# A hybrid attention and linear-attention layer on one core: the token scales stored once instead of tile by tile, and four weight roundings moved from VectorE to ScalarE

## The chip, the core and the metric

The kernel runs on one core of a Trainium2 chip. The metric is the device time of one execution in microseconds (us). Engines are named as in the profile: PE is TensorE (the matrix unit), DVE is VectorE, ACT is ScalarE, POOL is GpSimd, SP is SyncE. In this kernel SP issues every DMA.

## The reference

One inference step of one layer, for a prompt of 2048 tokens of width 1024 and for 32 sample tokens that continue another stream:

```
n = rmsnorm(x, g_mix)
z = n @ w_in                       # 1024 -> 2320 columns: qa 512, ka 128, va 128,
                                   # qg 256, kg 256, vg 512, rg 512, ca 16
A = sliding-window attention(qa, ka, va)     # chunks of 64, window 128, sinks, QK-norm
G = gated linear attention(qg, kg, vg, log_sigmoid(ca @ w_alpha + b_alpha) / 16)
G = rmsnorm(G) * silu(rg)
h = x + concat(A, G) @ w_out
y = h + relu(rmsnorm(h) @ w_up)^2 @ w_down   # 1024 -> 4096 -> 1024
```

Besides y, the last keys and values and the states of the linear attention are returned. All is float32. The RMS norm of a token is a number per token (the token scale, `rstd`) times the gain `g_mix` per column; the kernel multiplies the activations by the gain ahead of the projection and the products by the token scale behind it.

## The kernel before

The prompt is cut into 16 tiles of 128 tokens, and the 32 sample tokens are tile 16. A matrix product in float32 is made of three products of rounded parts: each operand is split into `hi` (rounded to the format of the fast matmul) and `lo` (the rest, rounded), and PE computes hi·hi + hi·lo + lo·hi. For a weight (`split_weight`, lines 195 to 208), SP loads a piece of 512 KB into a buffer `stage`, one engine rounds it to `hi` (ACT in line 203 or DVE in line 205), and another writes `lo` (POOL or DVE in line 207).

The kernel has three phases.

Attention takes up to some 392 us of the trace. Its tiles come in the order 0 to 9, 16 (sample), 10 to 15. For each tile, `front` (lines 252 to 275) loads the transposed tokens `xT1a` (512 KB), has DVE multiply them by the gain, ACT round them to `nT_h` and POOL write `nT_l`; `scales` (line 280) loads the tokens a second time (`x1a`) and has DVE compute the 128 token scales into column t of the tile `rstd`, which has 128 partitions and 17 columns; `store` (lines 282 to 288) writes to DRAM what the second phase reads again: the scales of the tile (line 285) and, after every second tile, `nT_h` and `nT_l` of two tiles (1 MB each). Then PE computes the projections of the tile (`zq`, `zkv`, `zr`), and the attention of the tile (`qTp`, `S`, `pT`, `O` on PE) follows as a task that is resumed between matmuls.

The store of line 285 takes one column of `rstd`: 128 partitions with 4 bytes each, written to a DRAM tensor `rs` of its own, of shape [128, 1]. The second phase needs the scales along the free axis, the same for all partitions: line 631 reads the tensor back as one row of 512 bytes, broadcast to 128 partitions of the tile `rb`. The products `kq` of the linear attention multiply by it (line 739).

Linear attention takes from 392 to some 760 us. Its weights (`wqg`, `wkg`, `wvg0`, `wvg1`, each of two pieces) are loaded by `prepare_gla` (line 612): `wqg`, `wkg`, `wvg0` after the projection of keys and values of tile 15, `wvg1` some work later. The table `GLA_ENG` (line 594) says who splits the two pieces of a weight: the first is rounded by ACT and its `lo` written by POOL; the second has both done by DVE. The feed-forward network takes the rest, up to the end.

What sets the order: PE's instructions are chained by hand in the order in which the program issues them (`_pe`), and tasks are resumed by an estimated clock that each matmul advances. The order on the other engines is made by a scheduler at build time. Every engine then works strictly in order. SP issues DMAs in order too, and a DMA is given one of 8 semaphores in rotation, so each DMA waits until the one issued 8 before it on SP has landed. Loads `xT1a`, `x1a`, `stage` and the tiles `sq` and `rg` share a pool of 5 buffers of 512 KB, so a load may also wait until the last reader of an older tile is done.

Of the kernel before, what the change touches and what calls it, by code (L numbers as in the profile page):

```python
# [9 lines left out]
F32 = mybir.dt.float32  # L10
F32R = mybir.dt.float32r
I32 = mybir.dt.int32
AF = mybir.ActivationFunctionType
# [6 lines left out]
P = 128  # L20
# [8 lines left out]
class Builder:  # L29
    def __init__(self, ctx, tc, a, o, nt=NT, ffn=True):  # L30
        self.ctx, self.tc, self.nc, self.a, self.o = ctx, tc, tc.nc, a, o
        self.nt, self.with_ffn = nt, ffn
        nc = self.nc
        self.V, self.S, self.G, self.T, self.Q = nc.vector, nc.scalar, nc.gpsimd, nc.tensor, nc.sync
        pool = lambda name, bufs, **kw: ctx.enter_context(tc.tile_pool(name=name, bufs=bufs, **kw))
        self.const = pool("const", 1)
        self.small = pool("small", 3)
        self.io = pool("io", 5)
        self.w = pool("w", 8)
        self.dram = pool("dram", 1, space=DRAM)  # L40
        self.psm = pool("psm", 3, space=PSUM)
        self.pss = pool("pss", 5, space=PSUM)
        tiles = list(range(nt)) + [nt]
        dt = lambda shape, name: self.dram.tile(shape, F32, tag=name, name=name)
        self.mixT = [dt([P, KB, self.rows(t)], f"mixT{t}") for t in tiles]

        self.nTd = [[dt([P, KB, 2 * P if t < nt else NS], f"nT{x}{t}") for x in "hl"] for t in range(0, nt + 1, 2)]
        self.cad = [dt([16, self.rows(t)], f"ca{t}") for t in tiles]
        self.rsd = [dt([self.rows(t), 1], f"rs{t}") for t in tiles]
        self.rgd = [dt([self.rows(t), 512], f"rgd{t}") for t in tiles]  # L50

        self.last_pe = self.last_table = None
        self.clock = 0.0
        self.state_clock = -1e9
        self.tasks = []
        self.seq = 0
# [174 lines left out]
    def attention_phase(self):  # L231
        tc, a, V, S, G, Q = self.tc, self.a, self.V, self.S, self.G, self.Q
        nt = self.nt
        w_in = a["w_in"].rearrange("(k p) n -> p k n", p=P)
        with ExitStack() as ctx:
            wx = ctx.enter_context(tc.tile_pool(name="wx1a", bufs=1))
            wk = ctx.enter_context(tc.tile_pool(name="wk1a", bufs=2))
            c = ctx.enter_context(tc.tile_pool(name="c1a", bufs=1))
# [14 lines left out]
            def front(t, xT=None):  # L253

                r = self.rows(t)
                xT = xT or load_xT(t)
                if t == nt:
                    nT[t] = (*(c.tile([P, KB, NS], F32R, tag=f"nTs{x}", name=f"nTs{x}") for x in "hl"), 0)
                elif t % 2 == 0:
                    nT[t] = (*self.tok_pair(f"nT_{t}", 2 * P), 0)  # L260
                else:
                    nT[t] = (*nT[t - 1][:2], P)
                h, l, off = nT[t]
                ts = slice(off, off + r)
                step = 2 if t == 0 else 4
                for k in range(0, KB, step):
                    ks = slice(k, k + step)
                    V.tensor_tensor(
                        out=xT[:, ks], in0=xT[:, ks], in1=self.gmix[:, ks].unsqueeze(2).broadcast_to([P, step, r]), op=ALU.mult
                    )  # L270
                    S.activation(h[:, ks, ts], xT[:, ks], AF.Copy)
                    (V if t in (0, nt) else G).tensor_tensor(
                        out=l[:, ks, ts], in0=xT[:, ks], in1=h[:, ks, ts].bitcast(F32), op=ALU.subtract
                    )

            def scales(t, x=None):

                r = self.rows(t)
                x = x or load_x(t)
                V.tensor_copy(self.rstd[:r, t : t + 1], self.rms(x, x, r, f"a{t}"))  # L280

            def store(t):

                r = self.rows(t)
                Q.dma_start(self.rsd[t], self.rstd[:r, t : t + 1])
                if t == nt or t % 2:
                    for x, dst in zip(nT[t], self.nTd[t // 2]):
                        Q.dma_start(dst, x.bitcast(F32))
# [3 lines left out]
            gm = slice(self.g0, self.g0 + KB)  # L292
            Q.dma_start(self.packed[:, gm], a["packed"][:, gm])
            V.memset(self.ones, 1.0)
            S.activation(self.rstd[:, :1], self.ones, AF.Square)
            front(order[0])
            wq = self.wide_pairs(w_in, 0, "wq", (("act", "dve", 2), ("act", "dve", 2)), (0,))
# [29 lines left out]
            def project_q(t):  # L327
                r = self.rows(t)
                rs = self.rstd[:r, t : t + 1]
                qk = wk.tile([P, 5, 2, 64], F32, tag="qk", name=f"qk_{t}", bufs=3)  # L330
                sq = self.io_tile(f"sq_{t}")[:, :640].rearrange("p (j v d) -> p j v d", j=5, v=2)
                ps = self.ps_m(f"zq_{t}")[:r]
                token_gemm(ps, t, wq)
                pv = ps.rearrange("p (v j d) -> p j v d", v=2, j=4)
                S.activation(qk[:r, 0:4], pv, AF.Copy, scale=rs)
                S.activation(sq[:r, 0:4], pv, AF.Square, scale=rs)
                return qk, sq
# [31 lines left out]
            def project_gate(t):  # L369

                r = self.rows(t)
                rg = self.io_tile(f"rg_{t}")[:r, :512]
                ps = self.ps_m(f"zr_{t}")[:r]
                token_gemm(ps, t, wr)
                V.tensor_scalar(out=rg, in0=ps, scalar1=self.rstd[:r, t : t + 1], scalar2=None, op0=ALU.mult)
                Q.dma_start(self.rgd[t], rg)
# [180 lines left out]
            for i, t in enumerate(order):  # L557
                for j in order[i + 1 : i + 2 + (nt in order[i + 1 : i + 2])]:
                    if j not in nT:
                        front(j)  # L560
                        scales(j)
                        store(j)
                if i == 0:
                    z = {j: project_q(j) for j in order[:2]}
                    z = {j: project_kv(j, *z[j]) for j in z}
                    with tc.issue_after(self.weights_in):
                        for j in order[:2]:
                            store(j)
                elif i > 1:
                    z[t] = project_kv(t, *project_q(t))  # L570
                if t == nt - 1:
                    self.prepare_gla(0)
                self.spawn(attend_sample(*z.pop(t)) if t == nt else attend(t, *z.pop(t)))
                if t != nt - 2:
                    project_gate(t)
                if t == nt - 1:
                    project_gate(t - 1)
                if t == nt:
                    self.load_gla_consts()
# [11 lines left out]
            self.finish()  # L591


    GLA_ENG = (("act", "pool"), ("dve", "dve"))

    def load_gla_consts(self):
        a, c, Q, V = self.a, self.mid, self.Q, self.V
# [14 lines left out]
    def prepare_gla(self, part):  # L612
        w_in = self.a["w_in"].rearrange("(k p) n -> p k n", p=P)
        if part == 0:
            self.wqg = self.cols_pair(w_in, 768, "wqg", self.GLA_ENG)
            self.wkg = self.cols_pair(w_in, 1024, "wkg", self.GLA_ENG)
            self.wvg = self.wide_pairs(w_in, 1280, "wvg", self.GLA_ENG, (0,))
        else:
            self.wvg += self.wide_pairs(w_in, 1280, "wvg", self.GLA_ENG, (1,))

    def gla_tokens(self, h, tiles):
        nt = self.nt
        pair = self.tok_pair(f"nTb_{h}", sum(self.rows(t) for t in tiles))
        rb = self.mid.tile([P, 288], F32, tag="rb", name=f"rb_{h}")
        off = 0
        for t in tiles:
            r = self.rows(t)
            if t == nt or t % 2 == 0:
                for x, src in zip(pair, self.nTd[t // 2]):
                    self.Q.dma_start(x[:, :, off : off + src.shape[2]].bitcast(F32), src)  # L630
            self.Q.dma_start(rb[:, off : off + r], self.rsd[t].rearrange("r o -> o r").broadcast_to([P, r]))
            off += r
        return pair, off, rb

# [810 lines left out]
```

## Time and profile before

| what | us |
|---|---|
| median of 3 runs | 2317.13 (2316.85 to 2319.09) |
| the profiled execution | 2316.26 |
| its span, first to last instruction | 2314.5 |
| PE busy in the span | 2253.7 (97%) |
| DVE busy | 1410.0 (61%) |
| ACT busy | 953.1 (41%) |
| POOL busy | 1197.4 (52%) |
| mean granted clock of PE | 0.98 of full speed |

The profile is of one execution. Busy time is the time in which an engine executes something. PE is busy nearly all of the span, so it is PE's idle time, 61 us in all, and the stretches in which its granted clock is low that other engines and DMAs can change. A row of a timeline gives the start, the duration and the instruction, and in brackets how long the engine was idle before it and what released it. That releaser is inferred: where the engine named had been done for long, another wait ended last.

### The profile page before, as it was taken

To read this page: it belongs to the slowest core of one execution; us is meant where nothing else is said; L and a number is where in the kernel's file an instruction comes from. 1 tells how busy PE (TensorE), PEld (TensorE's weight loads), DVE (VectorE), ACT (ScalarE), POOL (GpSimd) and SP (SyncE) were. 2 spreads that over 40 slices of the span, in tenths; PEclk is the share of its full clock that TensorE was granted. 3 is DMA by queue.
4 is the path that set the end of the run, shared out by engine and by line. 5 is a ranking of instruction groups with operands and counts; after the bars stand their busy time and mean duration, and the time that the engine had idled before them with its cause. 6 is when DMAs were issued, how large, how long until landed. Compare 5 with 4: busy or idle time off the path is not lost.

```text
span 2314.5 us, 39745 instructions
## 1 busy us (share of the span) xinstructions
PE 2253.7 (97%) x15389; PEld 2117.4 (91%) x15389; DVE 1410.0 (61%) x3631; ACT 953.1 (41%) x1953; POOL 1197.4 (52%) x995
## 2 busy tenths in 40 slices
PE   7999999899998999999999999999999999999999
PEld 5777776788877999999999999999999999999999
DVE  7666657688887755555553755555554755555555
ACT  3554445455562643333334533333334533333331
POOL 3221224333241396667765566666665386666662
PEclk9999999889988999999999999999999999999999
DMA  8654563221322423222236222222227122222221
GB/s 233 140 107 107 145 173 125 84 73 66 106 82 81 128 78 97 82 74 74 73 109 185 74 73 74 73 73 73 74 63 219 55 74 73 73 74 73 74 64 52
DMA packets 154301, 221.56 MB, mean 96 GB/s; under 512 B 38224, under 2 KB 114976, under 8 KB 150272
## 3 DMA queue, kind: packets, MB, share of 16 engines
q1 hardware_dynamic: 154112, 219.02, 32.2%
q8 instruction: 121, 1.98, 0.4%
q14 instruction: 68, 0.56, 0.1%
HBM read 180.08 MB, written 38.91 MB: 95 GB/s over the span
## 4 chain that ended last, share of the span: by engine, by line
PE 74%; DVE 12%; DMA 5%; POOL 3%; issue 3%; ACT 2%; SPq 1%; POOLq 0%; DVEq 0%; ACTq 0%
PE dn L112 30%; PE PS4B L112 4%; PE PS3T L112 4%; PE PS2T L112 4%; PE PA22T L112 4%; PE PA11B L112 4%; PE PA12B L112 4%; PE PS1T L112 4%; PE zq L112 3%; PE op L112 3%; PE zr L112 3%; DVE AT L892 2%; PE zkv L112 2%; PE zv L112 2%; PE O L112 1%
## 5 line engine op out<-in xcount | busy, mean ns | idle before, releaser
L1103 POOL TENSOR_TENSOR wu<-stage,wu 128x512 fp32r<-128x512 f32 x336 | 432.5, 1299 | 468.3 <-ACT wu L1102 456.6
L1279 DVE TENSOR_TENSOR y<-y,dn 128x360 f32<-128x360 f32 (+1 forms) x768 | 393.0, 514 | 228.4 <-PE dn L112 225.5
L1102 ACT ACTIVATE wu<-stage 128x512 fp32r<-128x512 f32 x336 | 206.2, 628 | 493.6 <-PE dn L112 213.5
L1105 POOL TENSOR_TENSOR stage<-stage 128x512 f32<-128x512 f32 x192 | 249.4, 1299 | 7.5
L1232 ACT ACTIVATE r<-PA11B 128x360 f32<-128x360 f32 (+1 forms) x48 | 22.1, 460 | 284.4 <-PE PA11B L112 284.4
L1217 DVE TENSOR_TENSOR PA12B<-PA12B,r 128x360 f32<-128x360 f32 (+1 forms) x48 | 25.3, 526 | 150.2 <-PE PA12B L112 150.2
L719 POOL TENSOR_TENSOR g<-g,ggla 128x512 f32<-128x512 f32 (+1 forms) x17 | 25.0, 1489 | 170.4 <-ACT g L120 170.4
L112 PE MATMUL PA22T<-T4h,wu 128*128 128x360 f32 (+1 forms) x384 | 101.5, 328 | 0.0
L112 PE MATMUL PS3T<-T3h,wu 128*128 128x360 f32 (+1 forms) x384 | 100.1, 323 | 0.1
L112 PE MATMUL PS4B<-B22h,wu 128*128 128x360 f32 (+1 forms) x384 | 100.2, 324 | 0.0
L112 PE MATMUL PS1T<-T1h,wu 128*128 128x360 f32 (+1 forms) x384 | 98.9, 321 | 0.0
L112 PE MATMUL PA11B<-B11h,wu 128*128 128x360 f32 (+1 forms) x384 | 98.8, 321 | 0.0
L112 PE MATMUL PS2T<-T2h,wu 128*128 128x360 f32 (+1 forms) x384 | 98.7, 320 | 0.0
L112 PE MATMUL PA12B<-B21h,wu 128*128 128x360 f32 (+1 forms) x384 | 98.7, 321 | 0.0
L892 DVE COPY_PREDICATED AT<-masks,A 64x64 f32<-64x64 int32 (+1 forms) x330 | 82.9, 253 | 13.7 <-PE A L112 3.8
L816 POOL TENSOR_TENSOR E<-cc 128x256 f32<-128x256 f32 (+1 forms) x117 | 68.3, 622 | 25.3 <-PE A L112 19.5
L506 ACT ACTIVATE P<-S,negm 128x192 f32<-128x192 f32 (+2 forms) x128 | 51.6, 417 | 51.1 <-DVE negm L501 31.6
L112 PEld LDWEIGHTS PA22T<-T4h,wu 128*128 128x128 f32 x384 | 70.1, 193 | 0.0
L112 PEld LDWEIGHTS PS3T<-T3h,wu 128*128 128x128 f32 x384 | 69.1, 190 | 0.5 <-ACT T3h L1135 0.5
L112 PEld LDWEIGHTS PS4B<-B22h,wu 128*128 128x128 f32 x384 | 69.0, 190 | 0.0
L112 PEld LDWEIGHTS PS1T<-T1h,wu 128*128 128x128 f32 x384 | 68.1, 188 | 0.0
L112 PEld LDWEIGHTS PS2T<-T2h,wu 128*128 128x128 f32 x384 | 68.1, 188 | 0.0
(1008 smaller groups left out, 7736.5 us busy)
## 6 DMA issues: line engine op xcount, KB each, us to landing
stage<-in_w_up SPq DMA_DIRECT2D x96, 512.0 KB, 4.2
stage<-in_w_down SPq DMA_DIRECT2D x96, 512.0 KB, 3.9
stage<-in_w_out SPq DMA_DIRECT2D x24, 512.0 KB, 5.2
xT1a<-in_xT_prompt SPq DMA_DIRECT2D x16, 512.0 KB, 7.5
stage<-in_w_in SPq DMA_DIRECT2D x16, 512.0 KB, 5.3
x1a<-in_x_prompt SPq DMA_DIRECT2D x16, 512.0 KB, 6.9
out_yT_prompt<-y SPq DMA_DIRECT2D x32, 180.0 KB, 4.4
m<-mixT SPq DMA_DIRECT2D x11, 512.0 KB, 4.5
```

What stands on the lines that cost most here:

```text
L112: self._pe(self.T.matmul(out, lhsT, rhs, start=start, stop=stop), ns)
L506: S.activation(Pt[:, u, :n], sp[:, jp], AF.Exp, bias=negm[:, ch, u : u + 1], scale=0.125, accum_out=rsum[:, ch, u : u + 1],)
L719: G.tensor_tensor(out=gv, in0=gv, in1=ggla[:r].unsqueeze(1).broadcast_to([r, 4, P]), op=ALU.mult)
L816: G.tensor_tensor(out=e4, in0=c4, in1=ref, op=ALU.subtract)
L892: V.copy_predicated(dst, mk.unsqueeze(1).broadcast_to([L // nh, 2, w // m, m]), src[r].rearrange("s p (n m) -> s p n m", m=m),)
L1102: self.after(S.activation(h, src, AF.Copy), after)
L1103: G.tensor_tensor(out=l, in0=src, in1=f32(h), op=ALU.subtract)
L1105: tt = lambda o, x, y, op: G.tensor_tensor(out=o, in0=x, in1=y, op=op)
L1217: tt = lambda out, x, y, op=ALU.add: V.tensor_tensor(out=out, in0=x, in1=y, op=op)
L1232: S.activation(r0, product(b, "A11", "B11"), AF.Copy)
L1279: V.tensor_tensor(out=yg[:, f, :], in0=yg[:, f, :], in1=ps, op=ALU.add)
```

## The change

The DRAM tensor of the scales becomes one tensor `rs` of 17 rows and 128 columns. The 17 stores of line 285 go. Instead the tile `rstd` is set to 1.0 as a whole at the start (the sample tile fills 32 of its 128 partitions), and after the projection of keys and values of tile 15, PE transposes `rstd` (128 x 17) into PSUM (17 x 128), ACT copies that to a tile `rsT`, and one DMA writes it to `rs`, 17 rows of 512 bytes. The 17 broadcast loads of `rb` read rows of `rs`.

Apart from this, `GLA_ENG` now has the second piece of each of the four weights rounded by ACT in place of DVE; DVE still writes its `lo`.

```diff
-        self.rsd = [dt([self.rows(t), 1], f"rs{t}") for t in tiles]
+        self.rsd = dt([nt + 1, P], "rs")
...
             def store(t):
-                r = self.rows(t)
-                Q.dma_start(self.rsd[t], self.rstd[:r, t : t + 1])
                 if t == nt or t % 2:
                     for x, dst in zip(nT[t], self.nTd[t // 2]):
                         Q.dma_start(dst, x.bitcast(F32))
...
             V.memset(self.ones, 1.0)
+            V.memset(self.rstd, 1.0)
...
                 if t == nt - 1:
+                    pt = self.ps_s("rsT")[: nt + 1, :P]
+                    self.tr(pt, self.rstd)
+                    rsT = c.tile([nt + 1, P], F32, tag="rsT", name="rsT")
+                    S.activation(rsT, pt, AF.Copy)
+                    Q.dma_start(self.rsd, rsT)
                     self.prepare_gla(0)
...
-    GLA_ENG = (("act", "pool"), ("dve", "dve"))
+    GLA_ENG = (("act", "pool"), ("act", "dve"))
...
-            self.Q.dma_start(rb[:, off : off + r], self.rsd[t].rearrange("r o -> o r").broadcast_to([P, r]))
+            self.Q.dma_start(rb[:, off : off + r], self.rsd[t : t + 1, :r].broadcast_to([P, r]))
```

The change moves instructions at three places that matter below. The first is SP at the start, from the stores of tiles 0 and 1 to the load of tile 2's tokens (`xT1a`; `ck`, `cv`, `wal`, `d`, `masks` are small constant loads). Before:

```order
L285 DMA rs_127<-rstd 128x1
L285 DMA rs_128<-rstd 128x1
L288 DMA nTh_92<-nT_0h 128x2048
L288 DMA nTl_93<-nT_0l 128x2048
L404 DMA ck<-in_cache_k 128x128
L405 DMA cv<-in_cache_v 128x128
L603 DMA wal<-in_w_alpha 16x256
L604 DMA d_2801<-in_resets 128x288
L605 DMA masks<-in_masks 128x224
L631 DMA rb_4265<-rs_127 128x128
L631 DMA rb_4265<-rs_128 128x128
L250 DMA xT1a_510<-in_xT_prompt 128x1024
```

And now, with the load of `gk` that precedes this piece in both kernels:

```order
L315 DMA gk<-in_g_k 128x128
L286 DMA nTh_92<-nT_0h 128x2048
L286 DMA nTl_93<-nT_0l 128x2048
L403 DMA ck<-in_cache_k 128x128
L404 DMA cv<-in_cache_v 128x128
L608 DMA wal<-in_w_alpha 16x256
L609 DMA d_2774<-in_resets 128x288
L610 DMA masks<-in_masks 128x224
L250 DMA xT1a_493<-in_xT_prompt 128x1024
```

The load of `xT1a` stood 8 places behind the store of `nTl`; it now stands 6 behind it and 8 behind the load of `gk`.

The second place is DVE at the end of the attention phase, where the first pieces of the linear attention's weights arrive (`wqgh`, `wqgl`, `wkgh`, `wkgl` are hi and lo of two weights; `ssqk`, `ca`, `qk` belong to the keys and queries of tile 15, `qT` and `caT` to tile 14). Before:

```order
L205 CAST wqgh<-stage 128x1024
L457 TENSOR_SCALAR qT_4011<-qTp_4000,packed 128x4x2x64
L396 COPY caT_4008<-kTp_4005 16x128
L207 TENSOR_TENSOR wqgl<-stage,wqgh 128x1024
L352 TENSOR_REDUCE ssqk_4032<-sq_3925 128x10
L350 TENSOR_SCALAR ca_4030<-zkv_3966,rstd 128x16
L205 CAST wkgh<-stage 128x1024
L353 TENSOR_SCALAR ssqk_4032<-ssqk_4032 128x10
L207 TENSOR_TENSOR wkgl<-stage,wkgh 128x1024
```

And now:

```order
L456 TENSOR_SCALAR qT_3979<-qTp_3968,packed 128x4x2x64
L395 COPY caT_3976<-kTp_3973 16x128
L207 TENSOR_TENSOR wqgl<-stage,wqgh 128x1024
L351 TENSOR_REDUCE ssqk_4000<-sq_3893 128x10
L349 TENSOR_SCALAR ca_3998<-zkv_3934,rstd 128x16
L352 TENSOR_SCALAR ssqk_4000<-ssqk_4000 128x10
```

The two roundings are gone from DVE, and `qT` of tile 14 no longer stands behind one of them; `wkgl` follows five small instructions later.

The third place is ACT in the same stretch (`pS` and `aT` are steps of tile 14's attention; `qk`, `sq`, `v` take the products `zkv` of tile 15; `kW` is its key tile). Before:

```order
L203 ACTIVATE wqgh<-stage 128x1024
L536 ACTIVATE pS_1_128_3993<-pT_1_128_3988 128x512
L536 ACTIVATE pS_1_64_3998<-pT_1_64_3995 128x256
L345 ACTIVATE qk_3924<-zkv_3966,rstd 128x128
L346 ACTIVATE sq_3925<-zkv_3966,rstd 128x128
L348 ACTIVATE v_4028<-zkv_3966,rstd 128x128
L203 ACTIVATE wkgh<-stage 128x1024
L467 ACTIVATE kW_4017<-kTp_4005 128x128
L549 ACTIVATE aT_4091<-O_3945 128x512
```

And now:

```order
L203 ACTIVATE wqgh<-stage 128x1024
L535 ACTIVATE pS_1_128_3961<-pT_1_128_3956 128x512
L535 ACTIVATE pS_1_64_3966<-pT_1_64_3963 128x256
L203 ACTIVATE wqgh<-stage 128x1024
L344 ACTIVATE qk_3892<-zkv_3934,rstd 128x128
L345 ACTIVATE sq_3893<-zkv_3934,rstd 128x128
L466 ACTIVATE kW_3985<-kTp_3973 128x128
L347 ACTIVATE v_3996<-zkv_3934,rstd 128x128
L575 ACTIVATE rsT<-rsT 17x128
L203 ACTIVATE wkgh<-stage 128x1024
L548 ACTIVATE aT_4064<-O_3913 128x512
L203 ACTIVATE wkgh<-stage 128x1024
```

ACT has the second pieces of `wqgh` and `wkgh` and the copy `rsT` between its steps of the attention.

Further on, SP issues the store of `rs` behind tile 15's `v_prompt` store, and the five loads of `rb` for tiles 16 and 0 to 3 directly after it and one weight load and one store (before, they stood far apart and earlier). Late in the linear attention the scheduler swaps some neighbours: on ACT, `kdT` of tile 15 now stands behind the rounding `wo_11h` and one copy `op`, ahead of which it stood. The feed-forward network's order stays as it was but for a few neighbours.

## Rows read from the trace of the kernel before

**Rows 1.** The stages: window; us; busy (count) of each engine; clock; DMA share; GB/s.

```profile
27.00:80.00 53.00, 47.64 (x266) 39.31 (x267) 37.84 (x139) 23.46 (x73) 16.76 (x25) 0.96 0.80 178
80.00:317.00 237.00, 237.00 (x1358) 182.33 (x1357) 150.38 (x583) 116.19 (x375) 56.41 (x96) 0.99 0.50 118
317.00:376.00 59.00, 52.41 (x304) 40.73 (x303) 41.05 (x108) 27.64 (x88) 21.35 (x22) 0.97 0.75 220
...
760.00:2314.50 1554.50, 1543.45 (x9671) 1539.54 (x9669) 862.27 (x1749) 585.89 (x1120) 972.12 (x679) 1.00 0.28 85
```

**Rows 2.** Waits of PE until 760 us: us in total, times, longest.

```profile
PE zq L112 <- ACT nT_2h L271: 2.3, 1, 2.3
...
PE pT L116 <- DVE qT L457: 1.9, 1, 1.9
...
PE zq L112 <- POOL nT_2l L272: 0.7, 1, 0.7
```

**Rows 3.** The chain of waits, 25 to 82 us: start us, us, what.

```profile
30.38 13.50 DMA nTl<-nT_0l
43.95 3.73 DMA xT1a<-in_xT_prompt
```

**Rows 4.** Windows, by stretches of a few us.

```profile
31.00:32.00 1.00, 1.00 (x9) 1.00 (x9) 1.00 (x1) 0.00 (x0) 1.00 (x1) 0.86 3.06 393
32.00:38.00 6.00, 6.00 (x40) 5.46 (x39) 5.61 (x24) 1.77 (x6) 3.24 (x9) 1.00 0.70 27
...
58.00:64.00 6.00, 6.00 (x44) 4.88 (x42) 4.23 (x21) 4.05 (x19) 1.18 (x4) 1.00 0.50 18
...
335.00:342.00 7.00, 7.00 (x48) 5.95 (x48) 2.59 (x9) 2.14 (x4) 0.00 (x0) 1.00 1.02 55
```

**Rows 5.** The seventeen stores of rs, line 285.

```profile
DMA to landing us min/median/max: 2.9/8.8/15.2
```

**Rows 6.** The store of the sample tile alone, at 206.65 us.

```profile
DMA to landing us min/median/max: 2.9/2.9/2.9
```

**Rows 7.** Timeline of DVE at the start: start us, us, line, [idle before <-releaser].

```profile
35.86 0.82 DVE L352 TENSOR_REDUCE ssqk<-sq 128x10 f32<-128x640 f32 x1 [0.32 <-ACT sq L346]
...
47.70 1.29 DVE L268 TENSOR_TENSOR xT1a<-xT1a,packed 128x512 f32<-128x512 f32 x2 [5.15 <-DMA xT1a<-in_xT_prompt]
...
75.78 1.29 DVE L268 TENSOR_TENSOR xT1a<-xT1a,packed 128x512 f32<-128x512 f32 x2 [3.45 <-DMA xT1a<-in_xT_prompt]
```

**Rows 8.** The chain of waits, 320 to 372 us.

```profile
329.23 16.51 DMA stage<-in_w_in
```

**Rows 9.** Timeline of ACT, 338 to 366 us.

```profile
344.26 1.06 ACT L203 ACTIVATE wqgh<-stage 128x1024 fp32r<-128x1024 f32 x1 [5.25 <-DMA stage<-in_w_in]
```

**Rows 10.** Timeline of PE, 342 to 364 us.

```profile
345.86 0.65 PE L112 MATMUL O<-pS,v 128*64 128x256 f32 x4 [1.89 <-ACT pS L536]
...
359.17 1.09 PE L116 MATMUL qTp<-packed,qk 128*128 128x128 f32 x4 [4.63 <-DVE es L383]
```

**Rows 11.** Timeline of DVE, 337 to 365 us.

```profile
345.84 2.54 DVE L205 CAST wqgh<-stage 128x1024 fp32r<-128x1024 f32 x1 [8.04 <-DMA stage<-in_w_in]
...
351.16 2.30 DVE L205 CAST wkgh<-stage 128x1024 fp32r<-128x1024 f32 x1
...
358.20 0.83 DVE L356 TENSOR_TENSOR qk<-qk,rsq_y_qk 128x640 f32<-128x640 f32 x1
...
363.40 0.69 DVE L205 CAST wvg0h<-stage 128x1024 fp32r<-128x1024 f32 x1 [1.16 <-PE zr L112]
```

**Rows 12.** Windows where the granted clock is low.

```profile
430.00:470.00 40.00, 34.66 (x346) 28.18 (x346) 28.01 (x103) 17.12 (x27) 4.85 (x8) 0.72 0.23 82
...
359.00:362.50 3.50, 3.33 (x11) 2.85 (x12) 3.14 (x11) 1.35 (x7) 1.61 (x2) 0.52 0.25 90
```

**Rows 13.** Timeline of DVE, 384 to 392 us.

```profile
387.52 0.29 DVE L739 SCALAR_TENSOR_TENSOR kq<-zq,rb 128x32 f32<-128x32 f32 x2 [0.25 <-issue]
```

**Rows 14.** Timeline of POOL, 338 to 366 us.

```profile
345.45 2.37 POOL L207 TENSOR_TENSOR wqgl<-stage,wqgh 128x1024 fp32r<-128x1024 f32 x1 [11.83 <-ACT wqgh L203]
```

## The prediction

> **What bounds the kernel now.** I read the stages by windows first. PE is busy all of 80 to 317 us, and 1543.45 of 1554.50 us from 760 us on [rows 1]. A shorter DVE or a quieter DMA queue can gain nothing there. The reader is to look at the two stretches next to them: 27 to 80 us, where PE idles 5.4 of 53 us, and 317 to 376 us, where it idles 6.6 of 59 [rows 1]. Then the waits of PE, which name the idle pieces of the first stretch: `zq` on nT_2h 2.3, `zq` on nT_2l 0.7, `pT` on `qT` 1.9, together 4.9 us [rows 2]. Then the chain of waits, which says what stands behind them.
>
> In the first stretch the chain goes through DMAs alone: the store of `nTl` takes 13.50 us to land, and only then is `xT1a` of tile 2 issued, which takes 3.73 us [rows 3]. That a store of 1 MB takes so long is explained by the queue: at 31 us it moves 393 GB/s, from 32 to 38 us 27 GB/s [rows 4]. What stands in the queue there, ahead of `nTh` and `nTl`, are the two stores of `rs`, 128 pieces of 4 bytes each. All seventeen such stores land in 8.8 us as a median and at most in 15.2 [rows 5], the one with only 32 pieces in 2.9 [rows 6]. So the time goes with the pieces, some (8.8 - 2.9) / 96 = 0.06 us for each (an estimate), and while they are worked off little else moves. It comes again at 58 to 64 us (18 GB/s) and at 335 to 342 us (55 GB/s) [rows 4], each time some us after such a store. DVE feels the first two as idle pieces of 5.15 and 3.45 us ahead of `xT1a` [rows 7].
>
> In the second stretch a load of `stage` takes 16.51 us [rows 8] and ACT waits 5.25 us for it ahead of `wqgh` [rows 9]; in ACT's order `pS` stands behind, so PE idles 1.89 us ahead of `O` [rows 10]. DVE is idle 8.04 us, then rounds `wqgh` in 2.54 and `wkgh` in 2.30 us, and the end of this chain is `qk` of tile 15 at 358.20 + 0.83 = 359.03 [rows 11]. `qTp`, which transposes `qk`, starts at 359.17, 4.63 us after the last `S` [rows 10]; the row names `es` as the releaser, but the operand is `qk`.
>
> **The change part by part.**
>
> *The start.* Two stores and, before `xT1a`, two loads of `rb` leave SP's queue. `xT1a` no longer waits for `nTl` to land, since the DMA 8 places ahead of it is now `gk`. SP reaches it after the small loads; what may hold it longer is a buffer of its pool, and the last reader of one there is `ssqk` of tile 1, done at 35.86 + 0.82 = 36.7 [rows 7]. With a queue that moves some 390 GB/s, 2 MB of stores issued at 30 us are through after 5.4 us. So `xT1a` is issued near 36.7 in place of 43.95 and lands by 36.7 + 3.73 = 40.4; DVE is free for it at 47.70 - 5.15 = 42.55. It is then DVE that sets when `nT_2h` and `nT_2l` are ready, 5.15 us earlier, and PE's idle 2.3 + 0.7 goes whole. The same for the second load: without the 6 us at 18 GB/s it lands at least 5 us before 75.78, DVE needs it 3.45 us earlier, and the 1.9 of `pT` goes. Term: -4.9 us. At the low end DVE, late by 2 us for other loads, keeps 1 us of it: -3.9.
>
> *80 to 317 us.* Most of the seventeen stores go from here; PE has no idle time to give. Term: 0.
>
> *End of attention.* Without the stretch of 7 us at 55 GB/s `stage` lands some 5.9 us earlier (7 x (1 - 55/393) = 6.0 with the rate of the start [rows 4], somewhat less beside other traffic). Then ACT's `wqgh` is done by 340, before `pS` is wanted at 345.86 - 1.89 = 343.97, and 1.89 goes. On DVE the chain from `wqgh` at 345.84 to the end of `qk` is 13.19 us long and nearly without gaps; without the two roundings it is 13.19 - 2.54 - 2.30 = 8.35. It can begin with `qT` by 343.97, so `qk` ends by 352.3. PE is through with `S` at 359.17 - 4.63 = 354.54 now [rows 10], and at 354.54 - 1.89 + 0.3 = 352.95 then. So the idle 4.63 goes, with 0.6 us in hand. After this idle piece the granted clock was at 0.52, near the lower level of 1.2 GHz, for 3.5 us, with PE busy 3.33 [rows 12]; at full clock that work takes 3.33 x 0.52 = 1.7, so 1.6 more is won if PE doesn't idle. Against it stands the transpose of `rstd`, one instruction on PE: no row shows 128 x 17; four transposes of `qk` take 1.09 at the low clock [rows 10], so it lies between 0.05 and 0.3; I take 0.3, for a PE that also turns to another operand. Term: -1.9 - 4.6 - 1.6 + 0.3 = -7.8 us. Its ends: -8.1 (nothing for the transpose) and -2.7 (the first rival).
>
> *ACT.* Four roundings of 1.06 us each [rows 9] come to it, 4.2 us. Its idle time hides them: 5.25 us at `wqgh` alone. If that cover is gone, `pS` and the softmax of tile 14 are late, which is the first rival.
>
> *DVE's memset, the store of `rs`, the loads of `rb`.* The memset (128 x 17) has no row; it is under the 0.69 us of a rounding 60 times its size [rows 11], and DVE waits for the first loads anyway: 0, at most 0.7. The store of 17 rows lands between the 2.9 us of 32 pieces and 8.8, and I take 2.9, as its pieces are the fewer. The `rb` loads wait for it, at some 350 us; the first reader is `kq` at 387.52 [rows 13], 12 us earlier then, so they have some 20 us in hand. On SP, stores of `rg` and `ca` and the load of `wvg1` stand behind the waiting `rb` loads for up to 8.8 us; nobody needs them before the decay of the first half. Cost: 0.
>
> *Linear attention.* The swaps of neighbours change who is first, not how much there is to do. I take 0, and bounds of +-3 us, a third of what one stretch of low clock costs there (9.7 us, worked out with the rivals).
>
> Sum: -4.9 + 0 - 7.8 = -12.7, from the profiled 2316.26 to 2303.6. The median of the runs shown, 2317.13, lies 0.87 above the profiled execution, so the forecast for the median is 2304.4.
>
> **A rule against it.** The Trainium skill, "Perfetto Trace Analysis", section "Optimizing Scalar/DVE Operations", says that an operation with a fast DVE mode is faster on DVE, and that moving it to ScalarE pays only where DVE is saturated. Rows: alone a rounding takes DVE 0.69 us and ACT 1.06, but 2.54 where POOL's `wqgl` (2.37 us) runs beside it [rows 9, 11, 14]. By the rule with the time of 0.69 DVE would shed 1.4 and not 4.84, and of my sum 3.4 would go, to 2307.8; the rows of this place carry 4.84. I count this case with the first rival.
>
> **The rivals.**
>
> *ACT takes DVE's place (2309.5).* If `stage` still lands late, ACT's roundings stand in its strict order between `pS`, `sq` and the softmax. Then the idle 1.89 stays and three more roundings, 3 x 1.06 = 3.2 us, come ahead of the softmax of tile 14. Term at the end of attention: -7.8 + 1.9 + 3.2 = -2.7; sum -7.6. For it: ACT already waits there for the DMA [rows 9]. Against it: the store that makes the stretch slow is gone.
>
> *The queue is slow for another reason (2308.2).* The stretch of 32 to 38 us also holds four small constant loads, and the stores might be victims. Then the 1.9 of `pT` and the 1.9 of `O` stay, while the issue of `xT1a` and the two roundings still gain: -(2.3 + 0.7) - 4.6 - 1.6 + 0.3 = -8.9. Against it: 2.9 against 8.8 us by pieces, and three stretches, two of them without constant loads. The Trainium skill, "DMA: Bandwidth & Descriptors", section "Anatomy of one DMA — SWDGE (gpsimd) path", gives some 2 us fixed for a DMA whatever its pieces, though for DMAs issued by GpSimd: by this a 512-byte store costs 2 us and this rival holds. The landings here, 8.8 us for 512 bytes, do not agree [rows 5].
>
> *No gain (2317).* `rb` lands after `kq` wants it, at 375 us or later, and PE waits again what it has won. It takes a delay of over 20 us on SP; the longest that one DMA holds anything up in the chains is 16.51 [rows 8].
>
> *Slower (2323.8).* Linear attention is where the clock falls after PE idles: 430 to 470 us at 0.72 with PE busy 34.66 [rows 12], so 34.66 x 0.28 = 9.7 us lost in such a stretch. The change brings other neighbours there, `kdT` of tile 15 behind a rounding that waits for a DMA among them. Two more such stretches cost 19.4: -12.7 + 19.4 = +6.7. It decides from 17.3 us on, where the gain and what can be told from no change are used up. Against it: the chains there hang on DVE, whose work stays.
>
> *More gain (2299.5).* The same stretch at full clock by half: -4.9 more.
>
> **How the numbers follow.** Forecast 0.52 (its own range 2301 to 2307.5), ACT in DVE's place 0.15, the slow queue for another reason 0.12, more gain 0.09, no gain 0.07, slower 0.05. A difference within 0.2%, 4.6 us, can't be told from no change by such runs. Faster: 0.52 + 0.15 + 0.12 + 0.09 = 0.88; same 0.07; slower 0.05. The range of 2299 to 2312 takes in the first three and most of the gain of the fourth, and leaves out about 0.17.
>
> **What would show it.** Right: no stretch under 100 GB/s at 32 to 38 and 335 to 342 us; `xT1a` of tile 2 issued by 38 us; PE without idle pieces of over 0.5 us in 28 to 355 us; `qTp` of tile 15 straight behind `S`; `kq` some 12 us earlier than 387.52. Wrong: `xT1a` waits for its buffer past 42 us; ACT idle ahead of `wqgh` still and PE ahead of `O`; `qTp` waits for `qk`; the end of linear attention no earlier than now though `kq` is.

## The result, and the profile after

The changed kernel takes 2303.86 us (median of 4 runs, 2300.71 to 2307.57), the kernel before 2317.32 in the same series: a ratio of 0.9941, 95% interval 0.9924 to 0.9958. A second series on another chip gave 2304.22 us and 0.9936 (0.9922 to 0.9951). Forecast was 2304.4 us. The profiled execution took 2304.6 us, its span 2302.8. (In later series two single executions, one of e5 below and one of the kernel before, took 3082 and 3088 us; neither is used.)

The stages by windows, to be laid beside [rows 1]:

```profile
27.00:80.00 53.00, 52.42 (x300) 43.57 (x300) 41.07 (x153) 26.11 (x84) 17.41 (x26) 0.94 0.50 178
80.00:310.00 230.00, 230.00 (x1319) 177.50 (x1318) 146.67 (x565) 113.42 (x364) 56.44 (x96) 1.00 0.34 120
310.00:365.00 55.00, 53.73 (x323) 41.81 (x322) 39.99 (x113) 31.74 (x95) 19.71 (x22) 1.00 0.75 248
...
748.00:2302.80 1554.80, 1542.54 (x9670) 1538.01 (x9668) 862.75 (x1749) 585.64 (x1120) 971.36 (x679) 1.00 0.28 85
```

PE idles 0.6 us in 27 to 80 us, where it idled 5.4, and 1.3 of 55 us at the end of attention, where it idled 6.6 of 59. The feed-forward network is unchanged. The waits of PE from 27.6 to 390 us, beside [rows 2]:

```profile
PE zkv L112 <- DVE rsq_y_a L184: 3.2, 1, 3.2
PE S L112 <- ACT P L505: 1.0, 2, 0.8
...
PE kTp L116 <- DVE es L382: 0.2, 1, 0.2
```

The waits of `zq` on nT_2h and nT_2l and of `pT` on `qT` are gone. Those ahead of `O` and `qTp` [rows 10] are too; new are 1.2 us ahead of `S` and `kTp`. The first row (idle time that ends at 27.6) was there before. SP's timeline at the start shows, at 34.67, the load that had been issued at 43.95 [rows 3]:

```profile
34.67 0.33 SPq L250 DMA_DIRECT2D xT1a<-in_xT_prompt  x1
```

The DMA queue in windows, beside [rows 4]. From 32 to 38 us it moves 277 GB/s where it moved 27. The four loads of `stage` at the end of attention are issued from 321 us on, before from 328; they run at 362 GB/s in the window below, while in the kernel before they ran into the stretch of 55 GB/s at 335 to 342 us. (In that same stretch the queue now moves 111 GB/s, as most of the loads are through.)

```profile
32.00:38.00 6.00, 6.00 (x38) 5.66 (x38) 4.72 (x13) 1.76 (x6) 3.53 (x9) 0.91 0.89 277
323.00:335.50 12.50, 12.50 (x80) 10.45 (x79) 6.92 (x27) 6.76 (x25) 4.18 (x7) 1.00 1.01 362
```

PE's timeline where it had idled 4.63 us [rows 10]; `qTp` of tile 15 now follows the matmuls without a gap:

```profile
346.28 0.39 PE L112 MATMUL zr<-wr0h,nT_14l 128*128 128x512 f32 x1
346.64 0.63 PE L116 MATMUL qTp<-packed,qk 128*128 128x128 f32 x4
347.49 0.30 PE L116 MATMUL kTp<-packed,kn 128*128 128x128 f32 x1 [0.23 <-DVE es L382]
```

Two marks divide the gain. `qTp` of tile 14 starts at 335.45 us, before at 341.68: 6.2 us are won by then. The first `kq`, at 387.52 before [rows 13], comes at 375.0:

```profile
L744 DVE SCALAR_TENSOR_TENSOR kq<-zq,rb x4: 180/303/414, 375.0 to 375.6; 128x32 f32<-128x32 f32 x2, 128x256 f32<-128x256 f32 x2
```

So 6.3 us more are won at the end of attention, 12.5 in all; the end of the span comes 11.7 us earlier. A second pair of profiles (b2 and r1 below) gives 6.0 us at the first mark and 15.1 at the second. The start is the same there; the end of attention gains 9.1, as the kernel before took longer in its second profile.

### The profile page after: what moved, and what is told of

It reads as the page before. It is cut to its first block, busy times and chain, and to the rows that moved or that the text cites. A ratio compares the mean times of both kernels' runs of the same rounds, so it can differ in the third digit from the quotient of the medians.

```text
span 2302.8 us, 39725 instructions
## 1 busy us (share of the span) xinstructions
PE 2250.9 (98%) x15390; PEld 2115.2 (92%) x15390; DVE 1407.0 (61%) x3628; ACT 956.1 (42%) x1958; POOL 1194.4 (52%) x995
## 4 chain that ended last, share of the span: by engine, by line
PE 80%; DVE 10%; POOL 4%; issue 3%; ACT 2%; DMA 1%; SPq 0%; POOLq 0%; ACTq 0%; DVEq 0%
PE dn L112 31%; PE zq L112 5%; PE op L112 4%; PE PS4B L112 4%; PE PA22T L112 4%; PE PS3T L112 4%; PE PS2T L112 4%; PE zr L112 4%; PE PS1T L112 4%; PE PA11B L112 4%; PE PA12B L112 4%; PE zkv L112 2%; DVE AT L897 2%; PE zv L112 2%; PE O L112 2%
## 5 line engine op out<-in xcount | busy, mean ns | idle before, releaser
L518 POOL TENSOR_TENSOR P<-P,es 128x512 f32<-128x512 f32 x15 | 15.6, 1040 | 101.9 <-ACT sq L345 43.0
```

What stands on the lines that cost most here:

```text
L518: (G if ch == 0 else V).tensor_tensor(out=dst, in0=src, in1=rb, op=ALU.mult)
```

## The experiments

Times are medians; ratios are to the kernel before on the same chip. The two marks, in us, are read from the profile of each run; where two stand, the second is that of a second profile.

| run | us | ratio (95%) | `qTp` 14 | first `kq` |
|---|---|---|---|---|
| before (two profiles) | 2317 to 2319 | 1 | 341.7 | 387.5, 389.5 |
| changed (two profiles) | 2303.86, 2304.22 | 0.9941, 0.9936 | 335.5, 334.9 | 375.0, 374.4 |
| e1 stored once only (two profiles) | 2310.84 | 0.9961 (0.9949 to 0.9973) | 334.7 | 377.5, 379.2 |
| e2 roundings only | 2314.18 | 0.9977 (0.9967 to 0.9987) | 342.0 | 386.2 |
| e3 changed + 4-byte stores | 2312.65 | 0.9970 (0.9959 to 0.9981) | 336.7 | 382.0 |
| e4 before, row stores | 2305.87 | 0.9943 (0.9931 to 0.9955) | 334.3 | 375.6 |
| e6 changed + last store | 2309.95 | 0.9966 (0.9954 to 0.9979) | 335.8 | 380.5 |
| e7 row stores + roundings on ACT | 2303.74 | 0.9937 (0.9920 to 0.9953) | 335.5 | 374.8 |
| e8 changed + stores, spaced | 2305.97 | 0.9951 (0.9936 to 0.9965) | 335.7 | 375.2 |
| e9 changed + stores of 64-byte pieces | 2303.81 | 0.9939 (0.9922 to 0.9955) | 336.3 | 375.8 |

**One part at a time.** e1 is the changed kernel with the old table of roundings, e2 the kernel before with the new one:

```diff
-    GLA_ENG = (("act", "pool"), ("act", "dve"))
+    GLA_ENG = (("act", "pool"), ("dve", "dve"))
```

> The scales stored once and transposed, the four roundings left on DVE. Theory (each part has a share; the 4-byte pieces hold the DMA queue, and DVE's two slow roundings hold qk of tile 15): all of the start's gain (PE idle 4.8 us and 1.6 us of low clock behind it) and the wait for pS (1.9 us) go, but DVE keeps a rounding of some 2.3 us in the chain to qk, so PE idles 2 to 4 us ahead of qTp of tile 15 with some low clock behind: 2307 to 2310 us. Rival A (the stores are all of it, the roundings cost nothing): 2304, as with both parts. Rival B (the roundings are most of it): 2311 or more.

> The kernel before with only the four roundings moved to ACT. Theory: nothing changes at the start (PE waits for zq and pT as before, 4.9 us); at the end of attention the loads of stage land late as before, PE waits 1.9 us ahead of O still, and its wait ahead of qTp shrinks from 4.6 to about 2 us: 2312 to 2315 us. Rival A: no difference from before, 2317. Rival B: the whole of the gain at the end of attention, 6 us or more: 2311 or less. If the parts add up, the gains of this run and of the one with the stores alone sum to 13.4 us.

The gains, 0.39% and 0.23%, add up to the 0.59 to 0.64% of both. By the marks of the first profiles the stores won 10.0 us of the attention phase and the roundings alone 1.3 (3.3 by the second profile of the kernel before). But the split is not a fixed one: e4 below keeps the roundings on DVE too, has no slow stores, and gains 0.57%. Both reach `qTp` of tile 15 some 12.5 us after that of tile 14 (12.4 and 12.9); behind it PE waits 1.25 us ahead of `kTp` and 0.8 ahead of `S` in e1, and not in e4.

The price of the roundings was not what I expected. DVE in e1, and POOL's `lo` of `wkg` beside it:

```profile
333.03 0.69 DVE L205 CAST wqgh<-stage 128x1024 fp32r<-128x1024 f32 x1 [2.21 <-DMA stage<-in_w_in]
...
338.22 0.67 DVE L205 CAST wkgh<-stage 128x1024 fp32r<-128x1024 f32 x1
...
340.08 2.34 DVE L179 TENSOR_SCALAR rsq_q_qk<-ssqk 128x10 int32<-128x10 int32 x1
```

```profile
339.09 3.31 POOL L207 TENSOR_TENSOR wkgl<-stage,wkgh 128x1024 fp32r<-128x1024 f32 x1
```

The roundings take 0.69 and 0.67 us, not 2.54 and 2.30: here they start 0.1 and 0.9 us ahead of POOL's `lo` of the same weight, where they started 0.4 and 0.6 us behind it. (In e4, whose loads come in time too, the first starts 0.4 us behind and takes 2.52.) In their place an instruction on 128 x 10 elements takes 2.34. In the changed kernel it is the same, on DVE and on POOL:

```profile
339.98 2.25 DVE L182 TENSOR_TENSOR rsq_q_qk<-rsq_y_qk 128x10 f32<-128x10 f32 x1
...
343.70 0.16 DVE L182 TENSOR_TENSOR rsq_q_qk<-rsq_y_qk 128x10 f32<-128x10 f32 x1
```

```profile
339.79 2.42 POOL L207 TENSOR_TENSOR wkgl<-stage,wkgh 128x1024 fp32r<-128x1024 f32 x1
```

The instruction that DVE starts while POOL's `lo` runs ends with it: at 342.23 beside 342.21 in the changed kernel, at 342.42 beside 342.40 in e1. The same line takes 0.16 us at 343.70, when POOL is idle. The Trainium skill, "SBUF — State Buffer", section "SBUF: two separate sides", calls the port pair that the two share an exclusive lock, so that the loser waits for the whole instruction; these rows agree.

**The stores put back.** e3 is the changed kernel with a store of 4-byte pieces at each old place, to tensors nobody reads; e6 has that of tile 15 alone:

```diff
             def store(t):
+                Q.dma_start(self.rsx[t], self.rstd[: self.rows(t), t : t + 1])   # e6: only for t == nt - 1
```

> The changed kernel with the seventeen stores of 4-byte pieces put back at their old places, to DRAM tensors that nobody reads. Theory (the pieces hold the queue whoever needs them): stretches under 60 GB/s come back behind the stores, xT1a of tile 2 and of the fourth tile late, PE idle ahead of zq or pT and ahead of O or qTp: 2310 to 2315 us. Rival (what hurt was only the order on SP, that xT1a stood 8 places behind the store of nTl and behind two loads of rb): 2304.

> The changed kernel with one store of 4-byte pieces put back, that of tile 15, ahead of the loads of stage (to a tensor nobody reads). Theory (each stall is paid where it falls; 80 to 317 us pay nothing): the start is that of the changed kernel, at the end ACT waits for stage, PE waits 3 to 5 us ahead of rsT or O: kq 3 to 6 us later than 375.0, in all 4 to 6 us over the changed kernel. Rival (the stall at the end is made by the nT stores and the tokens' loads, not by this store): kq as in the changed kernel, same time.

In e3 PE waits again, 4.3 us at the end, ahead of `rsT`, which now stands in front of `O`, and 1.6 for `pT`; the waits for `zq` do not come back:

```profile
PE rsT L117 <- ACT pS L537: 4.3, 1, 4.3
...
PE pT L117 <- DVE qT L458: 1.6, 1, 1.6
```

In e6 it is the second of these alone:

```profile
PE rsT L117 <- ACT pS L538: 3.4, 1, 3.4
```

The one store of tile 15 brings `kq` 5.5 us later, all seventeen 7.0. The stores of tiles 0 and 1 cost nothing here: `xT1a` of tile 2 is issued at 35.05 us although the queue stalls behind them (25 GB/s from 32 to 36 us), as it no longer stands behind `rb` and 8 places behind `nTl`.

**The same places, other pieces.** e4 is the kernel before with rows of 512 bytes (one scale copied along a row, so the linear attention takes each tile's first scale); e7 adds the new table:

```diff
+                rows[t] = self.small.tile([1, P], F32, tag="rsr", name=f"rsr_{t}", bufs=1)[:, :r]
+                V.tensor_copy(rows[t], self.rstd[:1, t : t + 1].broadcast_to([1, r]))
...
-                Q.dma_start(self.rsd[t], self.rstd[:r, t : t + 1])
+                Q.dma_start(self.rsd[t], rows[t])
```

> The kernel before, with each of the seventeen stores writing one row of 512 bytes (128 copies of the tile's first scale, made by one small DVE copy) in place of 128 pieces of 4 bytes; the loads of rb, the count of DMAs and nearly all places on SP stay. The linear attention thus works with the first token's scale for a whole tile. Theory (pieces): the stores land in 2 to 3 us, nTl by 37 us, and the time is that of the run with the stores once and the roundings on DVE: 2307 to 2310. Rival (a store costs its slot, semaphore and fixed time, whatever its pieces): 2316 to 2318.

> The kernel before with row stores (as in the run e4, scales of the first token of each tile for the linear attention) and the four roundings on ACT. Theory: with stage in time DVE has slack, and the roundings on DVE are worth the 2.0 us that PE still waits ahead of qTp of tile 15 in e4: the wait goes, kq at 372 to 374 us in place of 375.6; the median 1 to 3 us under e4's, 0.9925 to 0.994 of before. Rival A (the roundings are worth the 5 us of the run with them alone): 0.992 or less. Rival B (worth nothing any more): 0.9943, qTp still waits.

With all its DMAs, and with the roundings on DVE, e4 gains what the changed kernel gains, more than I expected. `xT1a` still follows the two loads of `rb` on SP and is issued at 36.10 us. So it takes both, the stall and the place behind it, to make PE wait for `zq`; the wait for `pT` comes with the stall alone (e3). The moved roundings take away most of the 2.0 us that PE waits ahead of `qTp` in e4 (0.3 are left). From the first mark to the second e4 takes 41.3 us and e7 39.3; `kq` comes only 0.8 us earlier, as e7 is 1.2 late at the first mark, and the ratios of e4 and e7 can't be told apart. With the scales stored once the same stretch takes 42.8 and 42.7 us (e1) and 39.6 and 39.5 (changed). So in the attention phase the roundings are worth 2.0 to 3.2 us once the stall is gone.

**What makes a store slow.** e5 drops the transpose and writes `rstd` to `rs` in 2176 pieces of 4 bytes. e8 and e9 are e3 with other targets: pieces 512 bytes apart, and pieces of 64 bytes side by side.

```diff
-                    Q.dma_start(self.rsd, rsT)
+                    Q.dma_start(self.rsd.rearrange("t p -> p t"), self.rstd)          # e5
...
+                Q.dma_start(self.rsx[t][:, :1], self.rstd[: self.rows(t), t : t + 1])  # e8, rsx[t] is 128 x 128
+                Q.dma_start(self.rsx[t], self.rstd[: self.rows(t), :16])               # e9, rsx[t] is 128 x 16
```

> The changed kernel without the transpose on PE and the copy on ACT: one DMA writes rstd (128 x 17) straight into rs (17 x 128), in 2176 pieces of 4 bytes; the scheduler places it ahead of the four loads of stage. Theory (the pieces are worked off one by one, some 0.058 us each for the whole queue): the store lands after about 126 us, nearly everything behind it on SP waits, PE idles 100 us or more at the end of attention: 2390 to 2440 us. Rival (a DMA has a fixed cost, or the pieces cost only in small DMAs): landing in 3 to 15 us, 2303 to 2312.

> The changed kernel with the seventeen stores of 128 pieces of 4 bytes put back as in e3, but each piece to a row of its own: the DRAM tensor that nobody reads is 128 x 128 and the store writes its first column, so two pieces lie 512 bytes apart in place of 4. The store of 2176 pieces landed in 18.2 us, so a piece does not cost 0.058 us everywhere. Theory A (the pieces of one store are held up because they write next to each other, into the same few hundred bytes): landing 2 to 4 us as a median, no stretch under 60 GB/s behind them, the time of the changed kernel, 0.993 to 0.995 of before. Theory B (a store of 128 pieces of 4 bytes runs on few of the 16 DMA engines, or each piece under some size costs the same wherever it goes): landing 8 us or more, 0.996 to 0.998 as e3.

> As e3, but each of the 128 pieces has 64 bytes (16 columns of rstd), written side by side, 8 KB in all. Theory A (pieces that write into the same few bytes hold each other up): with 64 bytes a piece the overlap shrinks or goes, landing 2 to 5 us, 0.993 to 0.996 of before. Theory B (the number of pieces on few engines): landing 8 us or more as in e3, 0.996 to 0.998.

The landings of the stores (minimum, median, maximum, us) of e3, e5, e8 and e9:

```profile
DMA to landing us min/median/max: 3.0/8.2/17.3
```

```profile
DMA to landing us min/median/max: 18.2/18.2/18.2
```

```profile
DMA to landing us min/median/max: 1.3/1.8/9.2
```

```profile
DMA to landing us min/median/max: 1.4/1.8/9.7
```

A landing is counted from the issue, so it has in it what stands ahead in the queue. My 126 us for e5 were wrong by a factor of 7: seventeen times the pieces land in twice the time. PE waited 10.5 us for `pS` there, and the profiled execution, the only one used, took 2317.90 us. In e8 the same 128 pieces of 4 bytes, far apart, land in 1.8 us, and in e9 larger ones, side by side, do; from 32 to 38 us the queue moves 362 GB/s in e8 and 326 in e9. So neither the number of pieces nor their size alone makes the store slow, but 4-byte pieces written next to each other. By its access pattern e5 writes neighbours in time to different rows, which fits, but its order was not varied. Why neighbours hold each other up no row shows.

**Second profiles.** r1 is the changed kernel once more, b2 the kernel before, e1b the kernel of e1; the last two are for a difference behind `kq`.

> The changed kernel once more, for a second profile and beside the variants on one chip. Theory: 0.9935 to 0.995 of before; the first kq on DVE within 1 us of 375.0, the store of rs once as before; what differs between the two profiles behind 400 us is the size of what single profiles can't tell. Rival (the first profile was a lucky one): kq later than 377.

> The kernel before once more, for a second profile. So far, from the first kq on DVE to the end of the span, the kernels with the roundings on ACT took 1923.9 to 1929.8 us (nine profiles, mean 1927.7), those with the roundings on DVE 1927.0, 1932.8 and 1932.2; the two groups differ in the order of SP's loads of w_out at the end of linear attention. Theory (that order costs the second group some 3 us): 1929 to 1934 us here, first kq at 387 to 388. Rival (no difference, the three were chance): 1924 to 1929.

> The run e1 once more (scales stored once, roundings on DVE), for a second profile. Theory (the order of SP's loads of w_out costs this group some 3 us behind kq): 1929 to 1934 us from the first kq to the end; kq at 377 to 378.5, 2 to 3 us later than in the changed kernel. Rival (chance): 1924 to 1929 behind kq; or kq at 375 to 376, which would make the roundings worth nothing in the attention phase.

From `kq` to the end b2 takes 1929.6 us and e1b 1931.0, which makes five profiles with the roundings on DVE of 1930.5 on average against 1927.7 for nine with them on ACT. Two profiles of one kernel differ by up to 2.6, so this is likely and not shown. It would account for what the roundings gain beyond their 2.0 to 3.2 us in the attention phase. `kq` in the second profiles is up to 2 us from the first; in b2 and e1b it is later than I expected.

## Why the prediction was right, and which of its steps failed

- *The start, -4.9.* It came to 6.2, and to 6.0 in the second pair of profiles. The idle pieces went as said (5.4 to 0.6 in the window). What I left out is the low clock behind the wait of `pT`; at the end of attention I had counted such a loss. Windows of the kernel before, with PE busy and the clock (third and eighth figure):

```profile
77.00:80.00 3.00, 2.21 (x9) 1.84 (x10) 1.96 (x8) 3.00 (x8) 2.77 (x3) 0.84 0.02 7
80.00:84.00 4.00, 4.00 (x18) 2.46 (x18) 2.49 (x12) 0.24 (x2) 0.00 (x0) 0.69 0.25 72
```

  2.21 x 0.16 + 4.00 x 0.31 = 1.6 us; with the 4.8 of idle time that makes 6.4. After the change the clock is 1.00 there. Against it, the clock stays low longer behind PE's first wait: from 28 to 34 us, by twos, it is 0.50, 0.50 and 0.74 in the changed kernel and was 0.50, 0.68 and 1.00, which takes back 0.9 us. So 5.5 of the 6.2 us are accounted for. Nor does every such wait bring a low clock: behind the 1.6 us for `pT` in e3 it stays at 1.00, and in the second profile of the kernel before it falls behind the waits for `zq` instead (0.73, 0.50 and 0.91 from 50 to 56 us).
- *80 to 317 us, 0.* Right: from 84 us on PE is busy throughout in e3 and in the changed kernel, with and without the stores, as before.
- *End of attention, -7.8.* It came to 6.3 in the first pair of profiles and to 9.1 in the second; the forecast lies between. In the first pair the 1.89, the 4.63 and the 1.6 of low clock went (-8.1); the transpose took at most 0.3, and 1.2 us of new waits came ahead of `S` and `kTp`: 6.6 by this sum. The new waits need not be ACT's roundings, as the first rival has it: e1, with these on DVE, waits 0.8 and 0.4 us ahead of `S` too, and e4 doesn't. What makes them stays open. That the sum of the forecast came out to within 1 us is in part luck: in the first pair the start won 1.3 us more than said and the end of attention 1.5 less.
- *The step that failed:* "without the two roundings it is 13.19 - 2.54 - 2.30 = 8.35". The idle 4.63 us went, but not for this reason alone. The 4.84 us were two instructions of 0.7 us each caught beside POOL's; without them another instruction was caught, for 2.25. From `qT` at 336.08 to the end of `qk` at 346.49 the chain took 10.4 us, and `qk` was 0.15 us ahead of `qTp` instead of 0.6. And more than half of the 4.63 goes with the stall: with the roundings still on DVE, PE waits only 1.96 us ahead of `qTp` in e4 and 1.19 in e1. That the whole of it went was in part luck. The 2.0 to 3.2 us that the roundings are worth there lie between the 4.84 and the 1.4 of the rule that I weighed (the Trainium skill, "Perfetto Trace Analysis", section "Optimizing Scalar/DVE Operations").
- *The second step that failed:* "some (8.8 - 2.9) / 96 = 0.06 us for each". It describes one column written into one row of 512 bytes and is no price per piece: 2176 pieces in another order land in 18.2 us, 0.008 for each, and 128 spaced ones in 1.8.
- *The queue slow for another reason*: refuted. e4 has every DMA of the kernel before and e8 a store at each old place, and both lose the stall. The rule of 2 us that the prediction takes from the Trainium skill ("DMA: Bandwidth & Descriptors", section "Anatomy of one DMA — SWDGE (gpsimd) path") fits the spaced and the larger pieces (1.8) and fails for neighbours (8.2).
- *Linear attention, 0 +-3.* -12.5 at `kq` became -11.7 at the end, within the bounds; in the second pair -15.1 became -14.9. Neither the slower rival nor "no gain" came: the loads of `rb` land in 3.3 us as a median, long before `kq`.

## What to carry to other kernels

Look for stores of a column, 128 pieces of 4 bytes into one row: they cost little themselves, but here the queue moved only 18 to 55 GB/s for 6 to 7 us behind them, and that is paid where an engine waits for a load. Three targets without 4-byte neighbours worked: rows of 512 bytes, 64-byte pieces, and pieces 512 bytes apart. And do not take the duration of an instruction that runs beside GpSimd as its price: here, when it was taken away, another one got the wait.

## What the runs showed of the hardware that I had not expected

128 pieces of 4 bytes land in 8.2 us (median) side by side and in 1.8 us when 512 bytes apart; 2176 of them, in an order that by the access pattern changes rows each time, in 18.2. Instructions on 128 x 10 elements on DVE took 2.25 and 2.34 us in place of under 0.2 while POOL subtracted 128 x 1024 elements. And a PE wait of 1.9 us cost 1.6 us more at a granted clock of 0.69 to 0.84 behind it in one profile, while a wait of 1.6 us in e3 cost nothing behind it.
